# MLP up projections as seven products of 2x2 blocks, with the activations passed through memory to a separate down phase

## The chip, the cores and the metric

The kernel runs on one core of one Trainium2 chip. The metric is the device time of one execution in microseconds (us), the median of several; lower is better. Engines: PE is TensorE, DVE is VectorE, ACT is ScalarE, POOL is GpSimd, and SP issues most of the DMAs.

## What is computed

One inference step of a two-layer decoder trunk with width 1024, for 1024 prompt tokens and 32 sample tokens (8 sequences of 4). Layer 0 has a state-space mixer, layer 1 an attention mixer with three branches. The change concerns what follows the mixer in both layers:

```python
D_MODEL = 1024
D_FF = 4 * D_MODEL
...
  even l: [u | z | xBC | dt] = RMSNorm(x) @ w_in_even
          x += concat(S5(u), SSD(z, xBC, dt)) @ w_out_even
  odd  l: [q | k,v_cmp | k,v_sel | k,v_win | gates] = RMSNorm(x) @ w_in_odd
          x += NSA(...) @ w_out_odd
  every l: x += relu(RMSNorm(x) @ w_up)^2 @ w_down
  final RMSNorm.
```

All inputs are float32. The up matrix is 1024 x 4096, the down matrix 4096 x 1024.

## The kernel before

Activations are kept transposed: 128 features on the partitions, the 1056 tokens in the columns, so that the width of 1024 is eight tiles. A column chunk `CH` has 352 tokens, three chunks make all of them.

**Matrix products.** Every float32 operand is split into a rounded part `hi` and a rest `lo` (type fp32r). `dense` (L375) multiplies a weight unit with the activations: for each chunk and each 128-row block `k` it issues three matmuls, `hi` x `hi`, `hi` x `lo` and `lo` x `hi` (L390 to L392), into one PSUM tile `mm` (4 buffers), and then calls `evac`. `w_load` (L308) loads the raw weights of a unit into one of two `w` tiles, `w_split` (L314) makes `hi` on ACT and `lo` on DVE in one of four `wh` tiles. All weights stand in one list `units`, and a unit is loaded two ahead and split one ahead.

**Tiles.** `slot` (L219) hands out one of 25 tiles of 128x1056, `xslot` (L234) one of the current phase's own, `half` (L249) one of eight of 128x512. A tile is handed on when all instructions that read it are done. The order of the instructions on each engine is laid out at build time from a simulated timeline, by the order of the program where it has a choice.

**The projection ahead of the MLP.** `ob_unit` (L1204, layer 0) and `oo_unit` (L2130, layer 1) compute output tile `d` of the mixer's projection and add the residual. `resid` (L1186) then squares it into `acc` (for the norm), scales it by the norm's gain and splits it into `xn[d]` (L1198 on ACT, L1199 on DVE). The norm's factor of each token isn't applied here.

**The MLP** (`mlp`, L1222). `up(f)` computes tile `f` of 32 of the up projection over all eight blocks and 1056 tokens; its evacuation takes relu on ACT, multiplies by the PSUM value on DVE (relu squared) and splits the result into `hh` and `hl` for the down projection. `down(G, d)` adds the products of four such tiles to output tile `d`, `Y[d]`. Up and down alternate: four up tiles, then the eight down parts of group `G`, eight times. `head` (L1226) computes the norm's factor: `ms_tok` sums `acc` over the partitions with matmuls of one column, `bcast_tok` spreads the result over the partitions with nine transposes; since relu squared is homogeneous, the factor `r2` is multiplied to `Y` once, after group 6 (L1264), and to the tiles of group 7. The last group goes chunk by chunk over all `d`, and `finish` makes the next layer's operands (`fin2` splits into `X2` by `resid`, and stores the residual to `res_d`) or the output (`fin4`).

Of the kernel before, what the change touches and what calls it, by code (L numbers as in the profile page):

```python
# [194 lines left out]
def _build(ctx, nc, tc, ins, outs, dbg):  # L195
# [35 lines left out]

    XBUFS = {"l0": (8, 1088), "mlp": (12, SLOT), "att": (11, 1088)}

# [7 lines left out]
    def px(name="px"):  # L241
        cnt[0] += 1
        return psum[-1][1].tile([128, 512], F32, name=f"{name}{cnt[0]}", tag="px", bufs=3 if psum[-1][2] == "att" else 4)

# [59 lines left out]
    units += mlp_units(1)  # L304
    raw, hl, wal = {}, {}, {}
    AHEAD = 300

    def w_load(i):  # L308
        if i < len(units) and i not in raw:
            ap, n = units[i]  # L310
            raw[i] = wslot(F32, "wr", "w", 2)
            (nc.gpsimd if 2 <= i < U_OB else nc.sync).dma_start(raw[i][:, :n], ap)

    def w_split(i, al=None):  # L314
        if i < len(units) and i not in hl:
# [94 lines left out]
    nc.scalar.dma_start(ssda, ins["ssd_a_log"].to_broadcast([128, 16]))  # L410
    xa = [(slot(F32R, "xh"), slot(F32R, "xl")) for _ in range(KD)]
    xr = [slot(F32, "x") for _ in range(KD)]
    for c in range(3):
# [764 lines left out]
    for i in range(8):  # L1178
        if YB[i] is None:
            YB[i] = slot(F32, "yb")  # L1180
            nc.sync.dma_start(YB[i][:, :NT], yb_d[i])
        YH.append(split(YB[i], g_ssd[:, i:i + 1], "yb", xslot(F32R, "ybh") if i < 6 else None))
        YB[i] = None
# [16 lines left out]

    X1 = {}
    acc1 = ptile(F32, "acc1", "big", 2, 1152)

    def ob_unit(d):  # L1204
        def evac(c, p):
# [3 lines left out]
            V.tensor_tensor(a, a, t[:, :CH], OP.add)  # L1209
            resid(d, c, a, g_mlp[:, d:d + 1], X1, acc1)  # L1210
            if c == 2:
# [9 lines left out]

    def mlp(l, X, acc, finish):  # L1222

        st = {"u": U_MLP[l], "H": {}, "Y": {}}

        def head():  # L1226
            r = ms_tok(acc, f"rm{l}")
            V.reciprocal(r, r)
            st["r2"] = bcast_tok(r, "r2")

        def up(f):
            b = {}

            def evac(c, p):
                if c == 0:
                    st["H"][f % 4, f // 4] = xslot(F32R, "hh"), xslot(F32R, "hl")
                hi, lo = (t[:, c * CH:(c + 1) * CH] for t in st["H"][f % 4, f // 4])
                t, h = half(F32, "rl"), half(F32, "h")
                S.activation(t[:, :CH], p[:, :CH], AF.Relu)  # L1239
                V.tensor_tensor(h[:, :CH], t[:, :CH], p[:, :CH], OP.mult)  # L1240
                if f // 4 == 7:
                    V.tensor_tensor(h[:, :CH], h[:, :CH], st["r2"][:, c * CH:(c + 1) * CH], OP.mult)
                S.copy(hi, h[:, :CH])
                V.tensor_tensor(lo, h[:, :CH], hi.bitcast(F32), OP.subtract)
            u = st["u"]
            st["u"] += 1
            return dense(u, X, range(KD), evac)

        def down(G, d):
            def evac(c, p):  # L1250
# [23 lines left out]

        cl = []
        for f in up(0):
            f()
        head()
        for G in range(8):
            for k in range(1, 4):  # L1280
                for f in up(4 * G + k):
                    f()
            if G < 7:
                for f in up(4 * G + 4):
                    f()
            if G == 7:
# [8 lines left out]
            for k in range(4):  # L1295
                del st["H"][k, G]

    new_phase("mlp")
    nc.sync.dma_start(outs["win_s"][:, 0:508], ins["state_win"][:, 4:512])
# [8 lines left out]
    mlp(0, X1, acc1, fin2)  # L1308

# [853 lines left out]
    def norm4(c):  # L2163
# [15 lines left out]
        for k in range(8):  # L2179
            V.scalar_tensor_tensor(YF[k][:, cc], YF[k][:, cc], g_fin[:, k:k + 1], p[:, :CH], op0=OP.mult, op1=OP.mult)  # L2180
            nc.sync.dma_start(outs["yT"][k][:, cc], YF[k][:, cc])

    new_phase("mlp")
    g_fin = param("norm_final")
    mlp(1, X3, acc3, fin4)
    psum.pop()[0].close()
# [39 lines left out]
```

## Time and profile before

| | us |
|---|---|
| median of 3 runs (lowest, highest) | 3232.7 (3230.3, 3233.6) |
| the profiled execution | 3231.5 |
| its span, first to last instruction | 3229.8 |
| TensorE busy | 3118.0 |
| DVE busy | 1793.2 |
| ACT busy | 1238.8 |
| POOL busy | 291.4 |

How to read it: busy is the time in which at least one instruction of the engine was under way. The MLP of layer 0 runs from 727 to 1473 us, that of layer 1 from 2468 to the end. "Clock" is TensorE's granted clock as a share of 2.4 GHz. Durations of matmuls overlap with one another, so the distance between starts tells their price.

### The profile page before, as it was taken

What the parts mean: (1) busy time and instruction counts of PE and PEld (TensorE: products, weight loads), DVE (VectorE), ACT (ScalarE), POOL (GpSimd) and SP (SyncE); (2) the same over time, 40 slices, a digit from 0 to 9 for tenths busy, and PEclk for the clock granted to TensorE, in tenths of its full rate; (3) what the DMA queues carried; (4) which work ended last, traced back from release to release, by engine and by line L of the source; (5) the groups of instructions that cost most, each with busy time, mean ns of one, the idle gap of its engine ahead of it and who ended that gap; (6) DMA issues with size and microseconds to landing.
All of it is one profiled execution on the core that took longest, in us unless ns stands there. A gap on an engine that the chain in (4) does not pass through costs nothing. (4 is left out here: it accounts for less than half of the span.)

```text
span 3229.8 us, 51519 instructions
## 1 busy us (share of the span) xinstructions
PE 3118.0 (97%) x20665; PEld 2953.8 (91%) x20665; DVE 1793.2 (56%) x3787; ACT 1238.8 (38%) x2463; POOL 291.4 (9%) x359
## 2 busy tenths in 40 slices
PE   7999998999999999999999998999999999999998
PEld 5999886999999999999999777777889999999998
DVE  4788787763233333576234777878854233333366
ACT  4223665433321112233236666666753322221112
POOL 0000000000000000001001344443410000000000
PEclk8999999999999999999999999999999999999999
DMA  5245343421111111217531122122143111111132
GB/s 181 93 130 156 108 130 130 142 93 53 46 46 46 45 45 45 87 63 245 154 96 57 17 66 60 33 48 48 14 137 100 46 46 46 46 44 44 45 99 74
DMA packets 172656, 259.09 MB, mean 80 GB/s; under 512 B 65072, under 2 KB 125712, under 8 KB 172352
## 3 DMA queue, kind: packets, MB, share of 16 engines
q1 hardware_dynamic: 142592, 194.80, 20.2%
q0 software_dynamic: 17728, 36.77, 4.5%
q10 hardware_dynamic: 12096, 24.22, 2.0%
q8 instruction: 163, 2.67, 0.3%
q14 instruction: 77, 0.63, 0.1%
HBM read 189.69 MB, written 57.62 MB: 77 GB/s over the span
## 5 line engine op out<-in xcount | busy, mean ns | idle before, releaser
L392 PE MATMUL mm<-xn,wh 128*128 128x352 f32 x1536 | 498.1, 324 | 0.0
L390 PE MATMUL mm<-xn,wh 128*128 128x352 f32 x1536 | 497.3, 324 | 0.0
L391 PE MATMUL mm<-xn,wh 128*128 128x352 f32 x1536 | 497.1, 324 | 0.0
L321 ACT CAST wh<-wr 128x1024 fp32r<-128x1024 f32 (+2 forms) x185 | 190.1, 1028 | 744.0 <-PE mm L391 727.8
L390 PE MATMUL mm<-hh,wh 128*128 128x352 f32 x1440 | 465.7, 323 | 0.0
L392 PE MATMUL mm<-hh,wh 128*128 128x352 f32 x1440 | 464.3, 322 | 0.0
L391 PE MATMUL mm<-hl,wh 128*128 128x352 f32 x1440 | 463.3, 322 | 0.0
L322 DVE TENSOR_TENSOR wh<-wr,wh 128x1024 fp32r<-128x1024 f32 (+2 forms) x185 | 221.3, 1196 | 303.5 <-ACT wh L321 303.5
L1258 DVE TENSOR_TENSOR Y<-Y,mm 128x352 f32<-128x352 f32 x336 | 174.3, 520 | 281.4 <-PE mm L392 280.4
L391 PEld LDWEIGHTS mm<-xn,wh 128*128 128x128 f32 x1536 | 290.2, 189 | 0.0
L392 PEld LDWEIGHTS mm<-xn,wh 128*128 128x128 f32 x1536 | 290.0, 189 | 0.0
L390 PEld LDWEIGHTS mm<-xn,wh 128*128 128x128 f32 x1536 | 289.6, 189 | 0.0
L391 PEld LDWEIGHTS mm<-hl,wh 128*128 128x128 f32 x1440 | 271.0, 188 | 0.0
L392 PEld LDWEIGHTS mm<-hh,wh 128*128 128x128 f32 x1440 | 270.8, 188 | 0.0
L390 PEld LDWEIGHTS mm<-hh,wh 128*128 128x128 f32 x1440 | 270.1, 188 | 0.0
L1944 POOL TENSOR_SCALAR P<-P,s,gates 128x640 f32<-128x640 f32 (+7 forms) x256 | 211.7, 841 | 274.9 <-DVE s L1940 225.0
L390 PE MATMUL mm<-xh,wh 128*128 128x352 f32 x672 | 224.9, 335 | 11.0 <-ACT xh L437 9.5
L391 PE MATMUL mm<-xl,wh 128*128 128x352 f32 x672 | 222.9, 332 | 3.4 <-DVE xl L438 3.4
L392 PE MATMUL mm<-xh,wh 128*128 128x352 f32 x672 | 222.0, 330 | 0.0
L1240 DVE TENSOR_TENSOR h<-rl,mm 128x352 f32<-128x352 f32 x192 | 99.7, 519 | 211.1 <-ACT rl L1239 210.7
L1986 PE MATMUL pv<-PT,vs 128*128 128x512 f32 x528 | 195.1, 438 | 11.7 <-ACT PT L1961 6.8
L1962 DVE TENSOR_TENSOR PT<-px,PT 128x512 fp32r<-128x512 f32 x264 | 176.9, 682 | 52.2 <-ACT PT L1961 51.4
(592 smaller groups left out, 6271.5 us busy)
## 6 DMA issues: line engine op xcount, KB each, us to landing
wr<-i_w_up SPq DMA_DIRECT2D x64, 512.0 KB, 3.5
wr<-i_w_dn SPq DMA_DIRECT2D x64, 512.0 KB, 3.5
wr<-i_w_in_e POOLq DMA_DIRECT2D x26, 512.0 KB, 4.3
res<-res SPq DMA_DIRECT2D x48, 176.0 KB, 2.3
csb<-cs_d SPq DMA_DIRECT2D x16, 512.0 KB, 7.0
gb<-ga SPq DMA_DIRECT2D x64, 128.0 KB, 3.3
x<-i_xT SPq DMA_DIRECT2D x24, 176.0 KB, 4.0
z_d<-z ACTq DMA_DIRECT2D x8, 528.0 KB, 2.7
```

Source lines behind the costliest of these rows:

```text
L321: S.copy(hi[:, :n], raw[i][:, :n])
L322: V.tensor_tensor(lo[:, :n], raw[i][:, :n], hi[:, :n].bitcast(F32), OP.subtract)
L390: T.matmul(o, wh, xh, start=(j == 0), stop=False)
L391: T.matmul(o, wh, xl, start=False, stop=False)
L392: T.matmul(o, wl, xh, start=False, stop=(j == n - 1))
L1240: V.tensor_tensor(h[:, :CH], t[:, :CH], p[:, :CH], OP.mult)
L1258: V.tensor_tensor(y[:, cc], y[:, cc], p[:, :CH], OP.add)
L1944: nc.gpsimd.tensor_scalar(P, P, b["s"][:, h:h + 1], GT[:, qb, gc:gc + 1], op0=OP.mult, op1=OP.mult)
L1962: V.tensor_tensor(lo, p, hi.bitcast(F32), OP.subtract)
L1986: T.matmul(PV[g, qb, i], v, t, start=(a == 0 and kb == 0 and k == 0), stop=False)
```

## The change

- `w_up` leaves the list of units; two up tiles `2p`, `2p+1` form a pair `p`, and their raw weights are loaded by `up_raw`. The 256 output rows of a pair x the 1024 input rows are seen as 2x2 blocks: output tile `2p` or `2p+1`, and input tiles of even or odd number. The tokens too are seen as two halves of 528 (`HF`). So the product is one of 2x2 blocks, and `mlp` forms it with seven block products (`PROD`) in place of eight: four sums of weight blocks (`s1` to `s4`, on POOL) and four of token blocks (`t1` to `t4`, in place, on POOL, `t1` of the later blocks on DVE).
- Each product is computed for two column chunks of 264 and four blocks `q`, three matmuls each, into PSUM banks A, B and C. p1, p6, p7 and p4 accumulate into the same bank, and ACT copies the state behind each of them to an `e` tile; DVE adds the other parts.
- `act` takes relu squared on DVE, multiplies by `r2` on POOL and stores the tile to memory (`h_d`).
- Behind all 16 pairs, the down phase runs by itself: `h_load(G)` loads four tiles of a group back and splits them, one group ahead. `r2` no longer multiplies `Y`.
- Tokens are prescaled: `resid_w` writes a single float32 tile `W["a"][d]`, multiplied by a factor per token (`W["s"]`) that comes from the mean square of the layer's input (`msx_d`, `m1x` for layer 0, `m1o` for layer 1), and `r2` takes it back. Token blocks of output tiles 0 to 3 are split (`b_split`) and summed (`b_sum`) during the projection, those of tiles 4 to 7 in `mlp`, four of them in `xslot` tiles of the MLP phase.
- The MLP phase has 5 `xslot` tiles in place of 12; in layer 0 all eight `ybh` tiles take `xslot`s.

The diff, cut to its core:

```diff
-    XBUFS = {"l0": (8, 1088), "mlp": (12, SLOT), "att": (11, 1088)}
+    XBUFS = {"l0": (8, 1088), "mlp": (5, SLOT), "att": (11, 1088)}
...
     def mlp_units(l):
...
+        return [(ins[f"w_dn{l}"][j], 1024) for j in range(32)]
...
         rB = half(F32, "rB")[:, :CH]
+        ms = half(F32, "msx")
+        V.tensor_copy(ms[0:1, :CH], p[0:1, :CH])
+        nc.scalar.dma_start(msx_d[:, cc], ms[0:1, :CH])
...
+    def b_split(W, n, q, al=slot):
+        t, x = al(F32R, "xw"), part(W, n, q)
+        hi, lo = t[:, :HF], t[:, HF:NT]
+        S.copy(hi, x)
+        V.tensor_tensor(lo, x, hi.bitcast(F32), OP.subtract)
+        W["x"][n, q] = hi, lo
...
+    def resid_w(d, c, src, g, W, acc):
...
+        V.scalar_tensor_tensor(W["a"][d][:, cc], src, g, W["s"][:, cc], op0=OP.mult, op1=OP.mult)
+        if c == 2 and d < 4:
+            for n in (("b21", "b22") if d % 2 else ("b11",)):
+                b_split(W, n, d // 2)
+            if d % 2:
+                b_sum(W, d // 2)
...
+    WX1 = {"a": {}, "x": {}, "s": bcast_tok(tok_scale(m1x), "sx"), "m1": m1x}
...
+        def prep(p, i):
+            n = ORDER[i]
+            t = wslot(F32R, "sw", "wh", 4) if i < 4 else ptile(F32R, "sw", "sw", 3, 1024)
+            hi, lo = t[:, :512], t[:, 512:1024]
+            x = sums(p, n) if n[0] == "s" else R[p][int(n[1]) - 1][:, int(n[2]) - 1]
...
+            S.copy(v(hi), x)
+            V.tensor_tensor(v(lo), x, v(hi).bitcast(F32), OP.subtract)
...
+        def act(x, f, j, c):
+            tok = slice(j * HF + c * 264, j * HF + (c + 1) * 264)
+            V.scalar_tensor_tensor(x, x, 0.0, x, op0=OP.max, op1=OP.mult)
+            nc.gpsimd.tensor_tensor(x, x, st["r2"][:, tok], OP.mult)
+            nc.sync.dma_start(h_d[l][f][:, tok], x)
+
+        PROD = {"p1": ("a11", "b11", "A", 1, 0), "p6": ("s2", "t2", "A", 0, 0), "p7": ("s3", "t3", "A", 0, 0),
+                "p4": ("a22", "t4", "A", 0, 1), "p5": ("s1", "t1", "B", 1, 0), "p3": ("s4", "b22", "B", 0, 1),
+                "p2": ("a12", "b21", "C", 1, 1)}
+
+        def prod(p, n):
+            wn, xn, bk, first, last = PROD[n]
+            for c in range(2):
+                if first:
+                    E[p, c, bk] = bank(bk, 3 if bk == "A" else 2)
+                o = E[p, c, bk]
+                wh, wl = SW[p, wn]
+                for q in range(4):
...
+                    T.matmul(o, a, xh, start=bool(first and q == 0), stop=False, skip_group_check=True)
+                    T.matmul(o, a, xl, start=False, stop=False, skip_group_check=True)
+                    T.matmul(o, b, xh, start=False, stop=(q == 3), skip_group_check=True)
+                if n in ("p1", "p6", "p7"):
+                    E[p, c, n] = e_t()
+                    S.copy(E[p, c, n], o)
...
+            if p < 15:
+                prep(p + 1, ORDER.index(wn))
+
+        def h_load(G):
+            for k in range(4):
+                t = xslot(F32, "hr")
+                nc.sync.dma_start(t[:, :NT], h_d[l][4 * G + k])
+                st["H"][k, G] = split1(t, "hh")
...
+        R[0], r = W["raw"], W["r"]
+        new_psum("up")
+        prep(0, 0)
+        prep(0, 1)
+        for n in ("b11", "b21"):
+            for q in (2, 3):
+                b_split(W, n, q, xslot if n == "b11" or q == 2 else slot)
+        prep(0, 2)
+        prep(0, 4)
+        for q in (2, 3):
+            b_split(W, "b22", q, xslot if q == 2 else slot)
+        for q in (2, 3):
+            b_sum(W, q, ("t1",), V)
+        for q in (2, 3):
+            b_sum(W, q, ("t3", "t2", "t4"))
+        prep(0, 3)
...
+        for n in ("t1", "t3", "t2"):
+            for q in range(4):
+                b_split(W, n, q)
+        st["r2"] = bcast_tok(r, "r2", xslot(F32, "r2"))
+        for q in range(4):
+            b_split(W, "t4", q)
...
+        for n in ("p1", "p2", "p5", "p6", "p7", "p4"):
+            prod(0, n)
+        for p in range(1, 16):
+            if p < 15:
+                R[p + 1] = up_raw(l, p + 1)
+            for n in ("p1", None, "p6", "p2", "p7", "p5", "p4"):
+                prod(*((p, n) if n else (p - 1, "p3")))
...
+        w_load(st["u"])
+        w_split(st["u"])
+        w_load(st["u"] + 1)
+        h_load(0)
+        prod(15, "p3")
+        W["x"].clear()
+        new_psum("mlp")
         for G in range(8):
-            for k in range(1, 4):
-                for f in up(4 * G + k):
-                    f()
             if G < 7:
-                for f in up(4 * G + 4):
-                    f()
+                h_load(G + 1)
```

## Rows read from the trace of the kernel before

**Rows 1.** The page, sections 1 and 2: busy shares; 40 slices of granted clock.
```profile
PE 3118.0 (97%) x20665; PEld 2953.8 (91%) x20665; DVE 1793.2 (56%) x3787; ACT 1238.8 (38%) x2463; POOL 291.4 (9%) x359
...
PEclk8999999999999999999999999999999999999999
```

**Rows 2.** Busy time by stretch: stretch, length, PE, PEld, DVE, ACT, POOL, clock, DMA, GB/s.
```profile
900.00:1000.00 100.00, 100.00 (x623) 100.00 (x623) 36.82 (x61) 20.47 (x33) 0.00 (x0) 1.00 0.13 43
```

**Rows 3.** The page, section 5: matmul groups of up (`xn`) and down (`hh`).
```profile
L392 PE MATMUL mm<-xn,wh 128*128 128x352 f32 x1536 | 498.1, 324 | 0.0
...
L392 PE MATMUL mm<-hh,wh 128*128 128x352 f32 x1440 | 464.3, 322 | 0.0
```

**Rows 4.** Timeline of TensorE where layer 0's MLP begins: start, duration, engine, line.
```profile
726.61 0.33 PE L392 MATMUL mm<-yb,wh 128*128 128x352 f32 x1
...
726.77 0.33 PE L390 MATMUL mm<-xn,wh 128*128 128x352 f32 x1
```

**Rows 5.** Timeline of TensorE where layer 0's MLP ends.
```profile
1473.20 0.33 PE L392 MATMUL mm<-hh,wx 128*128 128x352 f32 x1
1473.37 0.28 PE L1361 MATMUL mm<-wh,xn 128*128 128x256 f32 x1
...
1478.98 0.28 PE L1363 MATMUL mm<-wh,xn 128*128 128x256 f32 x1
```

**Rows 6.** Groups by form of DVE: count, busy us, mean ns, idle before.
```profile
L1033 DVE SCALAR_TENSOR_TENSOR yt<-xc,p_ssd_d,px 128x256 f32<-128x256 f32 x32 | 13.9, 475 | 3.9 <-PE px L1029 3.9
...
L1010 DVE TENSOR_TENSOR S<-S,px 128x256 f32<-128x256 f32 x28 | 11.7, 416 | 1.1 <-PE px L999 0.7
...
L987 DVE TENSOR_TENSOR xd<-xd,dts 128x512 f32<-128x512 f32 x16 | 11.0, 685 | 0.0
```

**Rows 7.** Groups by form of ACT.
```profile
L1255 ACT COPY Y<-mm 128x352 f32<-128x352 f32 x48 | 21.7, 452 | 51.4 <-PE mm L392 51.4
...
L2049 ACT COPY o<-pv 128x512 f32<-128x512 f32 x32 | 19.2, 600 | 18.8 <-PE pv L2047 18.5
```

**Rows 8.** Busy time by stretch, behind layer 0's MLP.
```profile
1475.00:1500.00 25.00, 25.00 (x213) 24.87 (x212) 10.71 (x55) 4.41 (x10) 5.76 (x6) 1.00 1.00 331
```

**Rows 9.** Groups by form of POOL.
```profile
L1944 POOL TENSOR_SCALAR P<-P,s,gates 128x512 f32<-128x512 f32 x32 | 25.8, 853 | 24.6 <-DVE s L1940 23.3 <-PE sc L1916 1.3
...
L1944 POOL TENSOR_SCALAR P<-P,s,gates 128x256 f32<-128x256 f32 x32 | 18.1, 580 | 27.9 <-DVE s L1940 22.5 <-PE px L1972 3.2 <-PE px L1693 2.1
```

**Rows 10.** One line of DVE: ns min/median/max, first and last start.
```profile
L1883 DVE TENSOR_TENSOR qhl<-qq,qhl x16: 679/688/1462, 1711.3 to 2319.5; 128x512 fp32r<-128x512 f32 x16
```

**Rows 11.** Timelines of DVE, then of POOL, around 1909 us.
```profile
1908.48 0.69 DVE L1962 TENSOR_TENSOR PT<-px,PT 128x512 fp32r<-128x512 f32 x1 [1.18 <-ACT PT L1961]
1909.09 1.46 DVE L1883 TENSOR_TENSOR qhl<-qq,qhl 128x512 fp32r<-128x512 f32 x1
...
1908.66 1.34 POOL L1944 TENSOR_SCALAR P<-P,s,gates 128x768 f32<-128x768 f32 x1
```

**Rows 12.** Timeline of TensorE behind `ms_tok` in layer 1.
```profile
2480.81 1.18 PE L352 MATMUL px<-csts,acc 128*128 128x1 f32 x10
...
2482.68 0.49 PE L390 MATMUL mm<-xn,wh 128*128 128x352 f32 x1
2482.97 0.49 PE L391 MATMUL mm<-xn,wh 128*128 128x352 f32 x1
...
2485.61 0.39 PE L391 MATMUL mm<-xn,wh 128*128 128x352 f32 x1
```

**Rows 13.** DMA issues: count, KB each, us from issue to landing.
```profile
res<-Y ACTq DMA_DIRECT2D x8, 528.0 KB, 5.9
...
yb<-yb_d SPq DMA_DIRECT2D x6, 528.0 KB, 7.1
```

**Rows 14.** Timeline of TensorE: the nine transposes of a token broadcast.
```profile
636.00 1.15 PE L365 MATMUL px<-csts,rs 128*128 128x128 f32 x9
```

**Rows 15.** Timeline of DVE in the first norm, from the PSUM sum.
```profile
16.87 0.52 DVE L429 TENSOR_SCALAR rB<-px 128x352 f32<-128x352 f32 x1
```

More of the change, by code (lines that the diff above doesn't have):

```diff
@@ L305, in _build @@
     raw, hl, wal = {}, {}, {}
+    held = {U_MLP[l] + i for l in range(2) for i in range(2)}
     AHEAD = 300
     def w_load(i):
-        if i < len(units) and i not in raw:
+        if i < len(units) and i not in raw and i not in held:
             ap, n = units[i]
@@ L314, in w_split @@
     def w_split(i, al=None):
-        if i < len(units) and i not in hl:
+        if i < len(units) and i not in hl and i not in held:
             w_load(i)
@@ L411, in _build @@
     xa = [(slot(F32R, "xh"), slot(F32R, "xl")) for _ in range(KD)]
+    msx_d = dp.tile([1, NT], F32, name="msx_d")
     xr = [slot(F32, "x") for _ in range(KD)]
@@ L1181, in _build @@
             nc.sync.dma_start(YB[i][:, :NT], yb_d[i])
-        YH.append(split(YB[i], g_ssd[:, i:i + 1], "yb", xslot(F32R, "ybh") if i < 6 else None))
+        YH.append(split(YB[i], g_ssd[:, i:i + 1], "yb", xslot(F32R, "ybh")))
         YB[i] = None
@@ L1199, in resid, with part @@
         V.scalar_tensor_tensor(lo, src, g, hi.bitcast(F32), op0=OP.mult, op1=OP.subtract)
-    X1 = {}
+    HF = NT // 2
+    h_d = [dp.tile([32, 128, NT], F32, name=f"h{l}_d") for l in range(2)]
+    PART = {"b11": (0, 0), "b21": (1, 0), "b22": (1, 1), "t1": (0, 0), "t3": (0, 1), "t2": (1, 1), "t4": (1, 0)}
+    def part(W, n, q):
+        k, j = PART[n]
+        return W["a"][2 * q + k][:, j * HF:(j + 1) * HF]
+    def b_split(W, n, q, al=slot):
[4 more added lines that the diff above has]
+        W["x"][n, q] = hi, lo
@@ new lines, in b_sum @@
+    def b_sum(W, q, ns=("t1", "t3", "t2", "t4"), eng=None):
+        x = {(k, j): W["a"][2 * q + k][:, j * HF:(j + 1) * HF] for k in range(2) for j in range(2)}
+        for n in ns:
+            o, a, b = {"t1": ((0, 0), (0, 1), (0, 0)), "t3": ((0, 1), (1, 1), (0, 1)),
+                       "t2": ((1, 1), (1, 1), (0, 0)), "t4": ((1, 0), (1, 0), (1, 1))}[n]
+            (eng or nc.gpsimd).tensor_tensor(x[o], x[a], x[b], OP.subtract)
+    def resid_w(d, c, src, g, W, acc):
+        cc = slice(c * CH, (c + 1) * CH)
+        if d == 0:
+            S.activation(acc[:, cc], src, AF.Square)
+        else:
+            t = half(F32, "sq")[:, :CH]
+            S.activation(t, src, AF.Square)
+            V.tensor_tensor(acc[:, cc], acc[:, cc], t, OP.add)
+        if c == 0:
+            W["a"][d] = slot(F32, "xa")
+        V.scalar_tensor_tensor(W["a"][d][:, cc], src, g, W["s"][:, cc], op0=OP.mult, op1=OP.mult)
[4 more added lines that the diff above has]
+                b_sum(W, d // 2)
@@ new lines, in tok_scale, with small9 @@
+    def tok_scale(m1):
+        r = small9("sc")
+        V.tensor_copy(r, m1)
+        rstd_of(r)
+        return r
+    def small9(n):
+        cnt[0] += 1
+        return cp.tile([128, 9], F32, name=f"{n}{cnt[0]}")
+    m1x = small9("m1x")
+    V.memset(m1x, 1.0)
+    nc.sync.dma_start(m1x[:, 0:8], msx_d[0, 0:TP].rearrange("(i p) -> p i", p=128))
+    nc.sync.dma_start(m1x[:TS, 8:9], msx_d[0, TP:NT].rearrange("(i p) -> p i", p=TS))
+    V.tensor_scalar(m1x, m1x, 1.0 / D, 1.0, op0=OP.mult, op1=OP.add)
@@ L1219, in _build, with up_raw @@
     nc.sync.dma_start(outs["conv"], convo.rearrange("p t k -> p (t k)"))
-    def mlp(l, X, acc, finish):
-        st = {"u": U_MLP[l], "H": {}, "Y": {}}
[L1226 to L1247, printed above, removed]
+    def up_raw(l, p):
+        o = []
+        for i in range(2):
+            t = wslot(F32, "wu", "w", 2) if p % 2 == 0 else ptile(F32, "wu", "wr", 2, 1024)
+            nc.sync.dma_start(t[:, :1024], ins[f"w_up{l}"][2 * p + i])
+            o.append(t[:, :1024].rearrange("p (q k f) -> p k q f", k=2, f=128))
+        return o
@@ L1296, in mlp @@
                 del st["H"][k, G]
+    WX1["raw"] = up_raw(0, 0)
+    WX1["r"] = ms_tok(acc1, "rm0")
     new_phase("mlp")
@@ L2181, in norm4 @@
             nc.sync.dma_start(outs["yT"][k][:, cc], YF[k][:, cc])
+    WX3["raw"] = up_raw(1, 0)
+    WX3["r"] = ms_tok(acc3, "rm1")
     new_phase("mlp")
     g_fin = param("norm_final")
-    mlp(1, X3, acc3, fin4)
+    mlp(1, WX3, acc3, fin4)
     psum.pop()[0].close()
```

82 lines of the change are left out of this document (63 added, 19 removed).

## The prediction

> **What bounds the kernel now.** I read the page first: TensorE is busy 97% of the span, with its clock at 9 tenths or more in nearly every slice [rows 1]. Then the busy time by stretch: inside the MLP of layer 0, 100 us hold 100.00 us of TensorE against 36.82 of DVE and 20.47 of ACT, POOL nothing, DMA at a 0.13 share [rows 2]. So in the two MLPs TensorE's instruction stream alone sets the pace; the others matter only where TensorE must wait for them. The groups say that a 352-column matmul "takes" 322 to 324 ns [rows 3], but these durations overlap; the price is the step from one start to the next. 623 starts in 100 us make 160.4 ns [rows 2]. At the two seams that the change touches there is no gap: the last matmul of the output projection starts at 726.61, the first of the up projection at 726.77 [rows 4]; the last down matmul at 1473.20, the next phase's first at 1473.37 [rows 5].
>
> **The up projections themselves.** Before: 32 tiles x 3 chunks x 8 blocks x 3 terms = 2304 matmuls a layer, 4608 x 160.4 ns = 739.1 us for both. After: 16 pairs x 7 products x 2 chunks x 4 blocks x 3 = 2688 a layer, 5376 of 264 columns. That is 7/8 of the columns in 7/6 of the instructions, so what a short matmul costs decides. No row has 264 columns; the nearest is 256, the dense run behind the MLP, 47 steps from 1473.37 to 1478.98, 119.4 ns [rows 5]. From 256 to 352 the step grows by 41.0/96 = 0.427 ns a column, so 264 columns cost 119.4 + 8 x 0.427 = 122.8 ns; 5376 x 122.8 = 660.2 us. **Term one: -78.9 us**, and a pair takes 168 x 0.1228 = 20.6 us. The bounds are narrow: 119.4 ns would give -97, the proportional 160.4 x 0.75 = 120.3 -92; 126 ns -62.
> The Trainium skill (TensorE: Matmul & The Clock Gate, Back-to-back issue gap) gives columns/2.4 + 2.5 ns, 149.2 and 112.5 ns here; that would make -82.7 us. The rows show 11 to 13 ns more per matmul than this page, so the rows decide.
>
> **The engines under a pair of 20.6 us.** DVE: 7 low halves of 512 columns at 0.685, 6 adds out of PSUM and 8 relu-squares of 264 columns at 0.43 and 0.49, from those of 256 at 0.416 and 0.475 [rows 6]: 4.8 + 2.6 + 3.9 = 11.3 us. ACT: 7 copies of 512 at 0.600 and 8 of 264 below 0.452 [rows 7]: 7.8 us. Each product waits for a copy out of the bank that it accumulates into (p6 for p1's copy, p7 for p6's, p4 for p7's); one and a half products lie between, 4.4 us for a copy of half a microsecond. DMA: 1.0 MB of weights and 1.1 MB of activations a pair are about 100 GB/s, and the trace moves 331 [rows 8]. All hidden. What the trace does not show is a two-input POOL operation, 4 of 512 and 8 of 264 columns a pair. One-input ones take 853 and 580 ns [rows 9]: 8.1 us a pair as lower end, 16.2 as upper end if the second input costs as much again. I take 1.4 times, 11.3 us. Here the row that speaks against the change is a DVE subtraction with both inputs in SBUF: usually 0.68 us, at most 1.46 [rows 10]; the long one starts at 1909.09, inside a POOL operation that runs from 1908.66 to 1910.00, and ends 0.55 us after it [rows 11]. The two exclude each other. DVE's such share of a pair is 4.8 + 3.9 = 8.7 us; 8.7 + 11.3 = 20.0, just under 20.6, and since a blocked operation needs 0.55 of its 0.685 afterwards, somewhat less. Preparation runs a pair ahead, so short blocks are absorbed; I charge **+6 us** for ACT standing behind a late POOL sum with PSUM copies queued after it (between 0 and the rival below).
> The Trainium skill (SBUF — State Buffer, Who interferes with whom) states that exclusion for a DVE instruction with two SBUF inputs against a POOL one that reads SBUF; this trace agrees (0.91 us of blocking). Its GPSIMD Engine Reference (Elementwise — side-by-side cycle accounting) gives 4497 ns for a two-input addition of 2048 columns; an estimate from that page is 9.1 us a pair, and the sum would keep its value.
>
> **The two heads.** Before, each up projection started on operands finished block by block during the projection before it. Now half of the token blocks (those from output tiles 4 to 7) can be split only into tiles of the new phase, whose memory is in use until the last projection matmul. DVE then has in hand: 4 operations of the last chunk (2.1 us), 22 splits and 2 differences of 528 columns at 0.70 (512 at 0.685, scaled [rows 6]) = 16.8, 5 weight halves = 3.4, 8 evacuations of the first products = 3.6: 25.9 us before p4's operands are complete. Operations back to back step by some 12% less than they last (1908.48 to 1909.09 for one of 0.69 us [rows 11]): 22.8. TensorE has five products to do ahead of p4, 14.7 us. So 8 to 11 us are uncovered. To that comes the clock: behind the single-column matmuls of `ms_tok` 352-column ones start every 0.29 us, twice the warm step and so the 1.2 GHz level, until about 2485.61 [rows 12]. That happens once per layer now; a head with waits should fall to it more than once, 1.7 us lost each. **+12 us per layer, +24.** Low end 3 each (all but the last chunk's chain hidden), high end 20 each (POOL's six sums exclude DVE on top, half clock throughout). A gain is excluded but for the present 1.7 us, since there is no gap to win.
>
> **Up to down.** Four activations are loaded back for the first down group; the fourth needs a tile whose last reader is p3 of pair 15, the last up matmul. A transfer of 528 KB lands in 5.9 us (a store) to 7.1 (a load) [rows 13], split about 1.2 on ACT and 1.4 on DVE: 8.5 to 9.7 us. With four PSUM tiles TensorE can do 4 x 9 matmuls on the other three, 5.8 us. **+4 per layer, +8**, between 0 (another tile comes free sooner) and 10 each. Later groups load 46 us ahead.
>
> **Smaller edits.** At the end of layer 0's down phase H, Y and the new X2 want 33 of 25 slots (H lay elsewhere before), so X2 of tiles 4 to 7 is written only as slots come free: c=0 some 1.7 us late, **+2** (0 to 7). Two more token broadcasts on TensorE, 1.15 us each [rows 14], and three copies in the first norm's chain, each at most L429's 0.52 [rows 15]: **+3**. The multiplication by r2 that leaves the down phase ran on DVE at a third load: nothing. The removed third DVE and second ACT step per up chunk: nothing, for the same reason.
>
> **Sum.** The profiled execution is 3231.5 us (span 3229.8 and 1.7 around it), 1.2 below the median. -78.9 + 6 + 24 + 8 + 2 + 3 = -35.9; 3195.6 by that execution, 3197 on the median.
>
> **Rivals.**
> 1. *Seams nearly free.* The order is laid out at build time from a simulated timeline and may pull sums and splits forward; heads 5 each, the rest half: 3232.7 - 78.9 + 10 + 4 + 1 + 3 + 0 = 3172. For it: half of the operands are split during the projection anyway. Against it: the memory of the other half.
> 2. *Slower: POOL and DVE become the bound of the up phase.* If POOL's second input costs as much as the first, 16.2 + 8.7 = 24.9 us a pair, 4.3 more than TensorE, x 32 = 138 us in place of the 6: 3329. It decides from 20.6 us on, POOL at 1.47 times the one-input rows without any overlap; 22 us a pair already undo the gain. For it: rows 11, and a sum of 20.0 that leaves 3%. Against it: 0.55 of 0.685, and two inputs need not double.
> 3. *Slower seams.* Heads and loads at their high ends, 40 + 20: 3232.7 - 78.9 + 60 + 7 + 5 + 6 = 3233.
> 4. *The change doesn't do what it says.* If a 264-column matmul steps at 137.5 ns or more (a floor per matmul and weight load), nothing is saved and the costs stay: 3276. Against it: 119.4 for 256 columns.
>
> **How the numbers follow.** Forecast 0.60 (3180 to 3215), rival 1 0.15, rival 2 0.13 (0.03 of it a mild form still faster), rival 3 0.07, rival 4 0.05. Likeliest: 3197. The range 3163 to 3240 takes in rivals 1 and 3 and the mild part of 2, and leaves the dear part of 2, rival 4 and a little below. About 0.2% is what a measurement here can tell from no change. Faster: 0.60 + 0.15 + 0.03 = 0.78; same, chiefly rival 3, 0.07; slower 0.15.
>
> **What would show it.** Right: some 814 starts of 264 columns per 100 us in the up stretches, clock 1.00 there; DVE busy near 55%, POOL near 55%; two gaps of 8 to 15 us in all at each head, ended by DVE splits of t2 and t4; one of a few us before the fourth reloaded activation. Wrong: fewer starts with TensorE waiting for ACT behind POOL in every pair (rival 2); an even step well above 123 ns (rival 4); heads with waits under 5 us (rival 1); TensorE waiting for loads beyond the first down group.

## The result, and the profile after

The changed kernel takes 3172.3 us (median of 4 runs, 3170.5 to 3178.0) against 3231.5 for the kernel before on the same chip: ratio 0.982, 95% interval 0.980 to 0.984. A second measurement, further down, gave 0.9817 (0.9801 to 0.9833). The forecast was 3197 in a range of 3163 to 3240: the sign was right and the range held, but the change brought 59 us where 36 were forecast. The profiled execution took 3170.7, its span is 3168.8.

The page of the changed kernel, to be set beside [rows 1]: TensorE does 80.7 us less, DVE 289 and POOL 493 us more, and the clock's slices look the same.

```profile
PE 3037.3 (96%) x21451; PEld 2871.4 (91%) x21451; DVE 2081.9 (66%) x4075; ACT 1290.5 (41%) x2575; POOL 784.0 (25%) x771
...
PEclk8999999999999999999999999999999999999999
```

Busy time by stretch inside the up phase of layer 0, the columns of [rows 2]: TensorE still never pauses, with 824 matmuls where 623 stood, while DVE and POOL are now busy two thirds of the time each.

```profile
900.00:1000.00 100.00, 100.00 (x824) 100.00 (x823) 69.94 (x103) 34.52 (x74) 66.38 (x59) 1.00 0.34 106
```

Such a count takes in the matmuls that were already under way when the stretch began. From the first to the last of the 822 that start in it the step is 121.8 ns; in the same stretch before, with 621 starts, it is 160.8 (the prediction took the count of 623 for starts, and 160.4 for the step).

Where the 61 us of span went is read by stages from TensorE's timeline: M0 is the time from the last output projection matmul of layer 0 to the first matmul behind layer 0's MLP, M1 that from the last projection matmul of layer 1 to the end of the span, "rest" is everything else. All kernels of this study, one profiled execution each:

| kernel | M0 | M1 | rest | span | median us (ratio, 95%) |
|---|---|---|---|---|---|
| before | 746.8 | 761.6 | 1721.5 | 3229.8 | 3231.5 |
| after | 716.2 | 730.8 | 1721.8 | 3168.8 | 3172.3 (0.982, 0.980–0.984) |
| after_again | 716.1 | 730.3 | 1719.9 | 3166.3 | 3171.0 (0.982, 0.980–0.983) |
| e1_sums_dve | 711.3 | 727.5 | 1723.7 | 3162.5 | 3164.3 (0.979, 0.977–0.980) |
| e9_w0_dve | 714.8 | 729.5 | 1722.5 | 3166.8 | 3166.9 (0.980, 0.978–0.982) |
| v1_head | 714.9 | 725.6 | 1724.0 | 3164.4 | 3168.1 (0.980, 0.978–0.981) |
| v3_both | 711.4 | 729.7 | 1727.0 | 3168.0 | 3168.7 (0.980, 0.978–0.981) |
| e3_r2_dve | 720.8 | 736.0 | 1728.1 | 3185.0 | 3187.9 (0.985, 0.983–0.987) |
| e2_pool_twice | 738.9 | 753.1 | 1726.0 | 3218.0 | 3219.8, one run |
| e4_load_late | 728.5 | 743.8 | 1723.2 | 3195.5 | 3197.3, one run |
| e5_short_cols | 697.9 | 714.8 | 1729.8 | 3142.5 | 3144.3, one run |
| e8_all_short | 690.9 | 707.7 | 1725.0 | 3123.6 | 3125.4, one run |
| e6_ybh_back | 723.6 | 730.3 | 1724.8 | 3178.7 | 3180.4, one run |
| e7_no_msx | 716.3 | 730.0 | 1718.7 | 3165.0 | 3166.8, one run |

The whole gain lies in the two MLPs, 30.5 and 30.8 us. The rest is unchanged within its scatter: it runs from 1719 to 1730 over kernels of which most have the same instructions there, so a few microseconds of it in a single profile mean nothing. M0 and M1 are steadier: after, after_again and e7_no_msx, whose MLPs are the same, have 716.1 to 716.3 and 730.0 to 730.8.

An MLP splits further. Its 2688 up matmuls at 121.8 ns make 327.4 us, where 2304 at 160.8 made 370.5: 43.1 less. So 12.6 of layer 0 and 12.3 of layer 1 are given back somewhere. The place is the head. In layer 0 the last projection matmul starts at 721.00, the first up matmul at 725.45, the first down matmul at 1066.36: 345.4 us for 327.4 of matmuls, 18.0 too many, nearly all of them before 755; the down phase has 0.4 over. Before, all overheads of that MLP together made 746.8 - 741.0 = 5.8. Timeline of TensorE at the two ends of the up phase:

```profile
721.00 0.32 PE L386 MATMUL mm<-ybh,wh 128*128 128x352 f32 x1
721.16 1.18 PE L346 MATMUL px<-csts,acc 128*128 128x1 f32 x10
723.62 0.98 PE L346 MATMUL px<-csts,acc 128*128 128x1 f32 x8 [1.28 <-DVE acc L1235]
725.45 0.36 PE L1355 MATMUL A<-xw,sw 128*128 128x264 f32 x1 [0.85 <-ACT xw L1215]
...
738.77 0.59 PE L1357 MATMUL C<-xw,sw 128*128 128x264 f32 x1 [6.12 <-DVE sw L1322]
739.16 0.42 PE L1355 MATMUL C<-xw,sw 128*128 128x264 f32 x1
739.38 0.42 PE L1356 MATMUL C<-xw,sw 128*128 128x264 f32 x1
...
1066.24 0.28 PE L1357 MATMUL B<-xw,sw 128*128 128x264 f32 x1
1066.36 0.32 PE L384 MATMUL mm<-hh,wh 128*128 128x352 f32 x1
```

At the start there are waits of 1.28, 0.85 and 6.12 us, and behind the long one the step is 0.22 us in place of 0.1218 until 742.68: the 1.2 GHz level, as in [rows 12]. It is 0.22 from 725.83 to 728.91 too, behind the single-column matmuls. At the end there is no gap at all. The head of layer 1 has the same long wait:

```profile
2455.17 0.59 PE L1357 MATMUL C<-xw,sw 128*128 128x264 f32 x1 [6.12 <-DVE sw L1322]
```

Busy time by stretch over the head, 720 to 760:

```profile
720.00:730.00 10.00, 7.87 (x52) 7.71 (x51) 9.43 (x19) 7.95 (x16) 1.90 (x2) 0.83 0.43 161
730.00:740.00 10.00, 3.88 (x28) 3.67 (x27) 10.00 (x7) 5.42 (x12) 10.00 (x7) 0.80 0.20 56
740.00:750.00 10.00, 9.04 (x60) 8.34 (x59) 10.00 (x14) 3.95 (x8) 3.34 (x2) 0.86 0.13 49
750.00:760.00 10.00, 9.50 (x77) 9.25 (x76) 9.39 (x18) 5.06 (x11) 5.85 (x4) 1.00 0.09 29
```

In the second stretch DVE and POOL are both busy all the time, and each gets through 7 operations. The timelines of DVE and of POOL show how:

```profile
733.55 1.79 DVE L1322 TENSOR_TENSOR sw<-wu,sw 128x512 fp32r<-128x512 f32 x1
735.26 1.75 DVE L1322 TENSOR_TENSOR sw<-sf,sw 128x512 fp32r<-128x512 f32 x1
736.94 1.78 DVE L1322 TENSOR_TENSOR sw<-wu,sw 128x512 fp32r<-128x512 f32 x1
...
733.02 1.76 POOL L1225 TENSOR_TENSOR xa<-xa,xa 128x528 f32<-128x528 f32 x1
734.75 1.72 POOL L1310 TENSOR_TENSOR sf<-wu,wu 128x512 f32<-128x512 f32 x1
736.43 1.74 POOL L1225 TENSOR_TENSOR xa<-xa,xa 128x528 f32<-128x528 f32 x1
```

They run in lockstep: every DVE subtraction, and every POOL sum, lasts 1.7 to 1.8 us, and one of each is done per 1.7 us. The DVE operation that ends at 738.72 is the weight half for which TensorE waits until 738.77.

### The profile page after: what moved, and what is told of

It is laid out like the page before. It is cut to its first block, busy times and chain, and to the rows that moved or that the text cites. A ratio compares the mean times of both kernels' runs of the same rounds, so it can differ in the third digit from the quotient of the medians.

```text
span 3168.8 us, 55263 instructions
## 1 busy us (share of the span) xinstructions
PE 3037.3 (96%) x21451; PEld 2871.4 (91%) x21451; DVE 2081.9 (66%) x4075; ACT 1290.5 (41%) x2575; POOL 784.0 (25%) x771
## 5 line engine op out<-in xcount | busy, mean ns | idle before, releaser
L384 PE MATMUL mm<-hh,wh 128*128 128x352 f32 x1440 | 465.1, 323 | 0.2 <-ACT c L1363 0.2
L386 PE MATMUL mm<-hh,wh 128*128 128x352 f32 x1440 | 464.9, 323 | 0.0
L385 PE MATMUL mm<-hh,wh 128*128 128x352 f32 x1440 | 464.5, 323 | 0.0
L315 ACT CAST wh<-wr 128x1024 fp32r<-128x1024 f32 (+3 forms) x121 | 122.9, 1016 | 468.8 <-PE mm L385 453.4
L1355 PE MATMUL A<-xw,sw 128*128 128x264 f32 x1024 | 291.7, 286 | 2.3 <-ACT xw L1215 1.6
L1357 PE MATMUL A<-xw,sw 128*128 128x264 f32 x1024 | 292.4, 286 | 1.0 <-DVE sw L1322 1.0
L1356 PE MATMUL A<-xw,sw 128*128 128x264 f32 x1024 | 293.0, 286 | 0.1
L385 PEld LDWEIGHTS mm<-hh,wh 128*128 128x128 f32 x1440 | 271.2, 188 | 0.0
L384 PEld LDWEIGHTS mm<-hh,wh 128*128 128x128 f32 x1440 | 270.7, 188 | 0.4 <-ACT c L1363 0.4
L386 PEld LDWEIGHTS mm<-hh,wh 128*128 128x128 f32 x1440 | 270.9, 188 | 0.0
L1338 POOL TENSOR_TENSOR e<-e,r 128x264 f32<-128x264 f32 x192 | 196.6, 1030 | 225.1 <-DVE e L1337 221.6
L316 DVE TENSOR_TENSOR wh<-wr,wh 128x1024 fp32r<-128x1024 f32 (+3 forms) x121 | 143.8, 1188 | 100.1 <-ACT wh L315 100.1
L2116 ACT ACTIVATE P<-sc,m 128x640 f32<-128x640 f32 (+7 forms) x256 | 180.1, 713 | 41.0 <-DVE m L2110 30.1
L1355 PEld LDWEIGHTS A<-xw,sw 128*128 128x128 f32 x1024 | 193.8, 190 | 2.9 <-ACT xw L1215 1.7
L1357 PEld LDWEIGHTS A<-xw,sw 128*128 128x128 f32 x1024 | 194.1, 190 | 1.4 <-DVE sw L1322 1.4
```

What stands on the lines that cost most here:

```text
L384: T.matmul(o, wh, xh, start=(j == 0), stop=False)
L385: T.matmul(o, wh, xl, start=False, stop=False)
L386: T.matmul(o, wl, xh, start=False, stop=(j == n - 1))
L1338: nc.gpsimd.tensor_tensor(x, x, st["r2"][:, tok], OP.mult)
L1355: T.matmul(o, a, xh, start=bool(first and q == 0), stop=False, skip_group_check=True)
L1356: T.matmul(o, a, xl, start=False, stop=False, skip_group_check=True)
```

## The experiments

**Is the head stretched by DVE and POOL, or by the amount of work?** Theory: the lockstep. Rival: DVE has so much to do that TensorE waits wherever the sums are made. The first experiment moves the sums of the later token blocks to DVE, which gives DVE more work and POOL less:

```diff
         for q in (2, 3):
-            b_sum(W, q, ("t3", "t2", "t4"))
+            b_sum(W, q, ("t3", "t2", "t4"), V)
```

> Only the six differences t3, t2, t4 of the later token blocks at each head move from POOL to DVE. Theory A (the head is long because DVE and POOL exclude each other: from 729.7 to 742 seven DVE operations and ten POOL ones alternate, each DVE step 1.70 us instead of 0.62): DVE gets 6 x 0.62 = 3.7 us more work and loses some 6 stalls of 1.1 us, so the 6.1 us wait of p2 for the low half of a12 falls below 3 us at each head, and the kernel gains 4 to 8 us: 3164 to 3168. Theory B (the head is long because DVE simply has 26 us of work before p4, as forecast): 3.7 us more work per head, 3180.

3164.3 us, 0.979 (0.977 to 0.980); the interval touches that of the changed kernel (0.980 to 0.984), so the stages have to tell. M0 falls by 4.9 and M1 by 3.3 us. The waits of TensorE in the head of layer 0 (engine, line, what it waited for: us in total, times, longest):

```profile
PE C L1357 <- DVE sw L1322: 2.2, 1, 2.2
PE px L346 <- DVE acc L1235: 1.3, 1, 1.3
PE A L1355 <- ACT xw L1215: 0.9, 1, 0.9
```

The long wait falls from 6.1 to 2.2, in layer 1 too, although DVE has six operations more. So the lockstep caused part of it. v3_both below holds the same edit: its M0 is the same, but its M1 is only 1.1 below the changed kernel's, so 3.3 is not firm. The second experiment was to take the other POOL work out of the head too, the weight sums of pair 0:

```diff
-            nc.gpsimd.tensor_tensor(ov, x, y, op)
+            (nc.gpsimd if p else V).tensor_tensor(ov, x, y, op)
```

> All POOL work in the two heads goes to DVE: the sums t3, t2, t4 of the later token blocks and the four weight sums of pair 0 (4 x 0.69 us more for DVE in each head). Theory A (the head is stretched by DVE and POOL excluding each other; what is left then is DVE's own backlog): the wait of p2 for DVE falls from 6.1 us to under 2.5, and the whole is 3160 to 3166 us, since nothing is left to exclude but the backlog grows by 2.8. Rival (the wait is only work that DVE has not reached yet, wherever the sums are made): DVE has 10 us more of its own to do per head, the wait grows and the whole is 3176 us or more.

The unaltered kernel ran beside it:

> The changed kernel, unaltered, on the same chip as e9_w0_dve, so that the two can be set side by side: 3170 to 3178 us.

After_again: 3171.0 us. With these sums on DVE as well: 3166.9, between the two theories' numbers but on the first one's side. Waits of TensorE in the head of layer 0:

```profile
PE A L1355 <- ACT sw L1321: 2.8, 1, 2.8
PE px L346 <- DVE acc L1235: 1.8, 1, 1.8
PE px L359 <- DVE rm L1433: 1.1, 1, 1.1
PE A L1356 <- DVE xw L1216: 1.0, 1, 1.0
```

The wait of p2 for DVE is gone, and undisturbed subtractions now start every 0.6 us (741.12, 741.74, 742.34 in DVE's timeline). But the edit doesn't do what its expectation says. In the changed kernel POOL had ended the weight sums of pair 0 ahead of the head (the last one is the first line here); now DVE does them behind the projection, and POOL does three sums of pair 1 in the head. Timelines of the changed kernel's POOL, then of this kernel's POOL, DVE and TensorE:

```profile
717.73 1.30 POOL L1310 TENSOR_TENSOR sf<-wu,sf 128x512 f32<-128x512 f32 x1 [0.95 <-POOL sf L1310]
...
735.44 1.60 POOL L1310 TENSOR_TENSOR sf<-sf,wu 128x512 f32<-128x512 f32 x1
737.01 1.72 POOL L1310 TENSOR_TENSOR sf<-wu,wu 128x512 f32<-128x512 f32 x1
...
735.84 1.76 DVE L1322 TENSOR_TENSOR sw<-sf,sw 128x512 fp32r<-128x512 f32 x1
...
734.51 0.56 PE L1355 MATMUL A<-xw,sw 128*128 128x264 f32 x1 [2.85 <-ACT sw L1321]
```

So some lockstep is left, and the first up matmul stands 7.6 us behind the last projection matmul, where it stood 4.5 behind in the changed kernel and in e1_sums_dve (in layer 1 9.7 in place of 3.8). These 3.2 us are nearly all of the 3.5 by which M0 is worse than in the first experiment. A head without POOL was therefore not measured. What is shown is that both theories hold a share: the lockstep's extra time, and beside it a true backlog of DVE. A third kernel left the sums of the later token blocks on DVE and interleaved sums and splits, so that each product's operands come just in time:

```diff
-        for q in (2, 3):
-            b_sum(W, q, ("t3", "t2", "t4"))
...
+        for q in (2, 3):
+            b_sum(W, q, ("t3", "t2"), V)
+        for q in range(4):
+            b_split(W, "t2", q)
+        prep(0, 3)
+        for q in range(4):
+            b_split(W, "t3", q)
+        st["r2"] = bcast_tok(r, "r2", xslot(F32, "r2"))
+        for q in (2, 3):
+            b_sum(W, q, ("t4",), V)
```

> As e1, and in the order in which the products need their operands: b11, b21, a12, then t1 and s1, then b22, t2 and s3, t3, t4; DVE does all differences of the later blocks. Theory A: each product's operands are ready when the product before it ends, but for the first 3 us; a head loses 4 to 6 us in all in place of 15: 3152 to 3160. Theory B (DVE's amount of work alone): as e1, 3175 to 3180.

3168.1 us, neither theory's number and not better than without the new order: M0 3.5 worse, M1 1.9 better than e1_sums_dve.

**Is POOL near to being the bound of the steady phase?** Rival 2 of the prediction. One kernel doubles POOL's multiplication and sends the copy to an unused tile, the other gives the multiplication to DVE (`V.tensor_tensor` for `nc.gpsimd.tensor_tensor`, not shown):

```diff
+            nc.gpsimd.tensor_tensor(half(F32, "dump")[:, :264], x, st["r2"][:, tok], OP.mult)
             nc.gpsimd.tensor_tensor(x, x, st["r2"][:, tok], OP.mult)
```

> POOL does each multiplication by r2 twice (the first result is left unused), 8 more operations of about 1.0 us a pair: 14.1 + 8.2 = 22.3 us of POOL against 20.4 us of TensorE. Rival 2 of the prediction, in its mild form (only POOL's own time counts): the up phases stretch to 22.3 us a pair, +61 us, 3233. In its dear form (POOL and DVE's two-input operations add up: 22.3 + 7 or more): 29 us a pair, +280 us, about 3450. If the 1.0 us of one operation is mostly waiting that is absorbed, less than +20 us.

> The multiplication by r2 moves from POOL to DVE: POOL keeps 4 sums of about 1.5 us a pair in place of 14.1 us of work, DVE gets 8 x 0.4 us more and fewer stalls. If the up phases are bound by TensorE alone, their rate stays at 822 to 823 starts in 100 us and the time within 3 us of the changed kernel (3169 to 3175). If POOL and DVE hold TensorE back somewhere, the rate rises and the time falls by more than 5 us.

Busy time by stretch, 850 to 950, of the doubled one first and of the one on DVE second:

```profile
850.00:950.00 100.00, 95.87 (x781) 95.02 (x780) 67.57 (x95) 28.75 (x66) 93.10 (x94) 1.00 0.33 99
```

```profile
850.00:950.00 100.00, 100.00 (x824) 100.00 (x823) 77.65 (x143) 34.31 (x74) 26.62 (x20) 1.00 0.33 108
```

Doubled, POOL is busy 93% of the time, a pair takes 168 steps of 128.4 ns = 21.6 us in place of 20.5, and the kernel loses 48 us, between the mild form of that expectation and the absorbed case. TensorE waits for ACT's copies out of the bank, and ACT in turn for the weight sums of POOL (behind the added line 1338 the line numbers are one higher than in the changed kernel):

```profile
PE A L1356 <- ACT e L1361: 22.1, 18, 4.0
```

```profile
ACT sw L1321 <- POOL sf L1310: 41.1, 13, 4.0
```

The first row is TensorE in the up phase of layer 0, the second ACT from 850 to 950. That is the path of the prediction's +6, "ACT standing behind a late POOL sum": it exists; with POOL's own load it is empty, with 1.5 times that load it isn't. With the multiplication on DVE the steady rate stays at the same count of 824, DVE at 78%, so the miss of that expectation (16 us slower than the changed kernel, where at most 3 were expected) lies elsewhere: M0 and M1 grow by 4.6 and 5.2, in the heads. In the 40 us behind the first up matmul of layer 0 TensorE starts 181 up matmuls in place of 218, which at 121.8 ns is 4.5 us. There DVE has the backlog, and eight more operations a pair should add to it; that was not tried apart. The other 6 us are in the rest, within its scatter.

**Does the seam from up to down cost nothing, and why?** The forecast was +4 a layer, because the fourth activation tile loaded back was held to need memory that the last up product still reads. Here the load of the first group stands behind that product, and it takes tiles 28 to 31 in place of 0 to 3, so it computes another output. Tiles 30 and 31 come out of the last pair, so two of the four loads have to wait for its stores:

```diff
-        h_load(0)
         prod(15, "p3")
+        h_load(0)
...
-                nc.sync.dma_start(t[:, :NT], h_d[l][4 * G + k])
+                nc.sync.dma_start(t[:, :NT], h_d[l][4 * G + k if G else 28 + k])
```

> The first down group loads activation tiles 28 to 31 in place of 0 to 3 (so the output isn't the reference's), and its loads stand behind the last product: they cannot start before the last two pairs are stored. Theory A (the seam from up to down costs nothing in the changed kernel because the first group's tiles were stored 14 pairs earlier and the reload slots come free one after the other): here the chain add, relu-square, multiplication, store, load, split of about 0.4 + 0.5 + 1.0 + 3 + 5 + 2.5 us is open, 10 to 13 us per layer and some 3 us of half clock: 3193 to 3205. Theory B (the seam is covered by matmuls of other chunks whatever the loads do): within 6 us of 3172.

3197.3 us, 25 more than the changed kernel, M0 +12.3, M1 +13.0. TensorE's wait behind the seam of layer 0, here and then in the changed kernel:

```profile
PE mm L384 <- ACT hh L330: 7.4, 1, 7.4
```

```profile
PE mm L384 <- ACT c L1363: 0.2, 1, 0.2
```

Behind the 7.4 us TensorE runs at half clock for ten matmuls (0.29 us a step until 1089.07), and then waits once more, for ACT's copy out of PSUM; together this is 11.0 us in the down phase. The stretch behind the wait, and the second wait:

```profile
1086.00:1091.00 5.00, 4.85 (x21) 4.65 (x22) 4.64 (x4) 4.03 (x5) 0.00 (x0) 0.68 1.02 391
...
1093.66 0.43 PE L384 MATMUL mm<-hh,wh 128*128 128x352 f32 x1 [1.96 <-ACT Y L1397]
```

In the changed kernel all four tiles are there. The timelines of ACT, DVE and SP show their splits and the issue of the third load. The last split is over by 1063.6, 2.8 us ahead of the first down matmul:

```profile
1051.12 1.08 ACT L330 CAST hh<-hr 128x1056 fp32r<-128x1056 f32 x1 [3.67 <-DMA hr<-h_d]
1053.63 1.08 ACT L330 CAST hh<-hr 128x1056 fp32r<-128x1056 f32 x1 [0.63 <-DMA hr<-h_d]
1056.78 1.08 ACT L330 CAST hh<-hr 128x1056 fp32r<-128x1056 f32 x1 [1.80 <-DMA hr<-h_d]
1061.21 1.08 ACT L330 CAST hh<-hr 128x1056 fp32r<-128x1056 f32 x1 [1.85 <-DMA hr<-h_d]
...
1052.23 1.26 DVE L331 TENSOR_TENSOR hh<-hr,hh 128x1056 fp32r<-128x1056 f32 x1 [2.30 <-ACT hh L330]
...
1062.32 1.26 DVE L331 TENSOR_TENSOR hh<-hr,hh 128x1056 fp32r<-128x1056 f32 x1 [0.78 <-ACT hh L330]
...
1053.52 0.32 SPq L1388 DMA_DIRECT2D hr<-h_d  x1
```

The third load goes out at 1053.52, just as DVE ends the split of the first tile (1052.23 + 1.26). By these times the memory of a reloaded tile is free again once it is split, and the later loads need not wait for the last product.

**How far is 264 columns from the floor of a matmul?** Rival 4. Two, then all three matmuls of each term get 192 columns (but for the first of each accumulation, 6 of the 168 of a pair); the other 72 columns are left out of these sums. The edit of the first:

```diff
-                    T.matmul(o, a, xl, start=False, stop=False, skip_group_check=True)
-                    T.matmul(o, b, xh, start=False, stop=(q == 3), skip_group_check=True)
+                    T.matmul(o[:, :192], a, xl[:, :192], start=False, stop=False, skip_group_check=True)
+                    T.matmul(o[:, :192], b, xh[:, :192], start=False, stop=(q == 3), skip_group_check=True)
```

> Two of the three matmuls of each term in the up phases take 192 of the 264 columns (the products hi x lo and lo x hi of the other 72 columns are left out, so the output is less exact). Theory A (a matmul's step is columns x 0.43 ns + about 8 ns): 121.5 - 72 x 0.43 = 90.5 ns for the short ones, a pair takes 56 x 121.5 + 112 x 90.5 = 16.9 us; the up phases fall by up to 3.5 x 32 = 111 us, 3061, if POOL and DVE (14.1 us and more of work a pair) keep up; in dense stretches the steps are 90 to 91 ns. Rival 4 of the prediction (a floor per matmul and its weight load above 100 ns): short ones at 105 to 121 ns, 3115 to 3172.

> All three matmuls of each term in the up products have 192 columns (the first of each accumulation keeps 264); 72 columns of each chunk are left out of the sums. Theory A (a matmul with its own weights has a floor near 111 ns, as e5_short_cols suggests: (3 x 114.6 - 121.5)/2): about 890 starts in 100 us, near 112 ns, and 3118 to 3130 us in all. Rival (the step pays columns, 192/264 of the streaming part, 91.5 ns): 1090 starts in 100 us unless POOL and DVE stop it, and below 3060 us.

Busy time by stretch of the one, then of the other:

```profile
900.00:1000.00 100.00, 100.00 (x873) 100.00 (x871) 72.90 (x110) 36.55 (x79) 70.93 (x64) 1.00 0.32 111
```

```profile
900.00:1000.00 100.00, 100.00 (x895) 100.00 (x894) 77.98 (x114) 37.08 (x80) 72.36 (x64) 1.00 0.34 117
```

From start to start the step is 115.0 ns on average with two short ones, so a short one takes (3 x 115.0 - 121.8)/2 = 111.6; with nearly all short the step is 112.1 ns. At the 0.43 ns a column that [rows 2] and [rows 5] give, 72 columns fewer would have made 90.8. There is a floor of about 112 ns, then, while TensorE waits for no other engine. The nine transposes of [rows 14] fit it: with 128 columns they start every 110 ns (636.00 to 636.88). The floor would be met near 264 - (121.8 - 112)/0.43 = 241 columns (an estimate); the change's 264 lie just above. The Trainium skill (TensorE: Matmul & The Clock Gate, LDWEIGHTS (loading the stationary operand)) gives a weight load of 128 columns 128/1.2 = 106.7 ns. The measured floor lies 5 ns above that, so a weight load for every matmul may be the cause; no run here tries it by itself.

**The small edits.** One kernel gives two of the eight `ybh` tiles their old memory back, the other leaves out the three copies of the mean square in the first norm (the prescale is then the constant that `m1x` is set to), the last puts this and e1_sums_dve together:

```diff
-        YH.append(split(YB[i], g_ssd[:, i:i + 1], "yb", xslot(F32R, "ybh")))
+        YH.append(split(YB[i], g_ssd[:, i:i + 1], "yb", xslot(F32R, "ybh") if i < 6 else None))
...
-        ms = half(F32, "msx")
-        V.tensor_copy(ms[0:1, :CH], p[0:1, :CH])
-        nc.scalar.dma_start(msx_d[:, cc], ms[0:1, :CH])
```

> Undoes one small edit of layer 0: the last two ybh tiles are slots again. The changed kernel reaches its first projection matmul 5.0 us sooner than the kernel before, although nothing in the change aims at that. Theory A (the tile edit moves the schedule): the projection starts at 626 us again, 3177. Theory B (the mean-square copies or the token broadcast move it): at 621 us, 3172.

> Leaves the stored mean square of layer 0 out (the prescale factor of layer 0 is a constant instead; r2 takes it back, so the result is the same up to rounding). Theory A (the three copies in the first norm's chain cost 2.4 us at the start, where the first input matmul went from 23.5 to 25.9 us): first input matmul at 23.5 us. Theory B (the order in which the scheduler lays out the start): it stays near 25.9. The projection's start tells whether these copies also cause the 5 us gained behind: 626 us if so, 619 to 621 if not.

> Two edits that worked alone, together: the sums t3, t2, t4 of the later token blocks on DVE, and no copies of the mean square in the first norm (layer 0 then takes another factor source, so the output is not the reference's in its digits where m1x is used; it shows the price of the copies). Theory A (the costs add, since one lies at the two heads and the other at the start): 3158 to 3162 us. Rival (both only shift where the planner lets TensorE wait): 3163 to 3170.

With the old memory, M0 is 7.4 us longer (the first up matmul comes 8.4 us behind the last projection matmul, in place of 4.5). `ybh` probably occupies memory that the head's token blocks want; that was not tried further. The expectation's other part, that the output projection would start later, can't be judged: it starts at 625.97 there, but at 621.23 and 627.20 in two executions of the unaltered changed kernel. The same holds for the copies. Without them the first input projection matmul starts at 23.05, with them at 25.86 (after), 24.20 (e1_sums_dve) and 23.95 (e2_pool_twice), and without them again at 24.02 (v3_both). They cost 0 to 2.8 us; more can't be said. Without them the output projection starts at 624.15, between those two, so that part of the expectation stays open too. Together the two edits gave 3168.7, not the sum of their gains: M0 as in e1_sums_dve, M1 and rest not, and its runs lie between 3161.6 and 3169.9.

The fastest version found is e1_sums_dve, 3164 us; the intervals of v1_head, v3_both and e9_w0_dve overlap with its own, and those of the changed kernel touch it.

## Why the prediction was right, and where its steps failed

- **Matmuls (-78.9).** Right in kind, mis-sized: 121.8 ns against 122.8 forecast; 741.0 - 5376 x 0.1218 = 741.0 - 654.8 = **-86**. The line through 256 and 352 columns lies 1.0 ns too high at 264, 5.4 us over 5376 matmuls. The other 1.9 come from the 623 that was read as starts: 4608 x 0.1608 is 741.0, not 739.1. Also, the rows lie 10 to 11 ns above the formula that the prediction quotes, not 11 to 13.
- **POOL's price (11.3 us a pair).** Right: the shortest operations are 1.284 us for 512 columns and 0.745 for 264, 4 x 1.284 + 8 x 0.745 = 11.1. The rows by line (ns min/median/max, first and last start) show how much longer many of them last. That time is in the busy shares too, which is why DVE and POOL show 70 and 66% where 55 each were forecast:

```profile
L1310 POOL TENSOR_TENSOR sf<-wu,sf x15: 1284/1284/1473, 763.1 to 1043.4; 128x512 f32<-128x512 f32 x15
...
L1338 POOL TENSOR_TENSOR e<-e,r x93: 745/1098/3257, 750.6 to 1064.1; 128x264 f32<-128x264 f32 x93
...
L1322 DVE TENSOR_TENSOR sw<-sf,sw x64: 678/693/1798, 729.5 to 1053.4; 128x512 fp32r<-128x512 f32 x64
```

- **Steady phase (+6).** Failed: 0, TensorE never waits there. The step added DVE's 8.7 and POOL's 11.3 us and found 3% of room. They do not add up like that: in e2_pool_twice POOL has 8 x 0.745 = 6.0 us more, the sum is 25.8, and the pair takes 21.6. So at least 4.2 of DVE's 8.7 us overlap there.
- **Heads (+12 each).** Right in size (12.6 and 12.3 measured), half right in mechanism, so the size is in part luck. The DVE backlog, the two falls to half clock and the 6 us wait are there. But the forecast took DVE at its undisturbed pace and left POOL's sums for the high end, and it placed the waits at the splits of t2 and t4; the long one stands ahead of p2, at a weight half, in the lockstep. e1_sums_dve gains 4.9 and 3.3 us by taking POOL's token sums out (in v3_both 4.9 and 1.1), net of the work that DVE gets by it.
- **Up to down (+8).** Failed: 0. I held that the fourth reload waits for a tile that the last product reads. It was loaded and split 2.8 us before the first down matmul; the reloaded tiles before it came free as soon as they were split. The low end, "another tile comes free sooner", was the case. How dear a late tile can be, e4_load_late shows with two late ones: 12 to 13 us per layer, with half clock and a second wait behind the first. What one late tile would have cost was not measured.
- **Smaller edits (+5).** The two added broadcasts run ahead of the two output projections (from 628.93 and from 2335.53), so they lie in the rest, as the copies and X2 do. None of them can be told from its scatter, 1721.8 and 1719.9 against 1721.5.
- **Sum.** -86 + 24.9 = -61 against -35.9. Of the 25 us between forecast and result 7 are the matmuls, 8 the seam, 6 the steady phase, and the remainder the small edits.
- **Rivals.** Rival 1 gave 3172, the measured time, for another reason: it had the heads at 5 us each, and they cost 12; the matmuls and the free seam made up for it. Rival 2 is absent at POOL's own load; at 1.5 times that it costs 48 us, not 132. Rival 3 didn't occur (its terms add up to 3232, not 3233). Rival 4's floor is real, about 112 ns, and 264 columns clear it.

## What to carry to other kernels

A phase that TensorE bounds can take on a good deal of DVE and POOL work for nothing, here 70 and 66% of the time, but not at its head, where their backlog is on the path: there the change gives 12 us back. In a head, count DVE and POOL together wherever both read two inputs from SBUF, and try the POOL share on DVE. When a product is cut into more and smaller ones, find the floor of a single matmul first; by the estimate above, cutting below about 241 columns would bring nothing here.

## What the runs showed of the hardware

- DVE and POOL in lockstep: a DVE subtraction of 512 columns goes from 0.68 to 1.75 us and a POOL sum from 1.28 to 1.74 when both have a queue of such work; together they finish one of each per 1.7 us. One after the other would be 1.28 + 0.68 = 1.96, and DVE alone does a subtraction and a sum in 2 x 0.6 = 1.2. The Trainium skill (SBUF — State Buffer, Who interferes with whom) calls the port pair that the two share an exclusive lock, and has a DVE instruction with two SBUF inputs contend with a POOL one that reads SBUF; the trace agrees in kind (0.68 to 1.75 us), with some 0.25 us of overlap per pair of operations.
- A floor of about 112 ns per matmul of 192 columns with weights of its own, at clock 1.00, against 121.8 for 264 columns and 160.8 for 352.
- Two-input POOL operations: 0.745 us for 264 columns and 1.284 for 512 undisturbed, 1.3 and 1.5 times the one-input ones of [rows 9].
- The same kernel differs between executions in when the output projection of layer 0 starts, 621.23 and 627.20 us, with nearly the same total. Why wasn't tried.
